# A ring of transfers moved from unrolled code into a hardware loop, and three loops placed differently in instruction memory

## Chip, cores, metric

One core of one Trainium2 chip. The time is device microseconds (us) of one execution; lower is better. "Before" is the kernel before the change, "after" the changed one.

## The reference

```python
def reference(x):                       # x: (4, 4096, 4352) float32
    B, N, D = x.shape
    G = 8
    x_g = x.reshape(B, N, G, D // G)
    x_g = x_g - x_g.max(axis=-1, keepdims=True)
    exp = np.exp(x_g)
    out = exp / exp.sum(axis=-1, keepdims=True)
    return out.reshape(B, N, D).astype(np.float32)
```

A softmax over groups of 544 numbers, 16,384 x 8 of them. It reads 285 MB and writes 285 MB.

## The kernel before

64 tiles of 128 partitions x 2 rows (4352 KB, 34,816 contiguous bytes a partition) go through a ring of six buffers and are worked on in place. SyncE issues all transfers from unrolled code; VectorE takes the maxima and scales, ScalarE exponentiates and sums. A "row" s is half a tile; the loops of ScalarE and VectorE have one body for the 12 rows of the ring.

```python
    def loop(engine):
        return nc.Fori(
            0, turns, engines=OrderedEngineSet([engine.engine]), head_slot={engine.engine: 0})
    # ... [vector_max, vector_scale, scalar_exp: cut]
    def load(t):
        b = t % NT                                   # NT = 6
        if t >= NT:
            nc.sync.wait_ge(stored[b], 16 * (t // NT))
        nc.sync.dma_start(out=bufs[b][:, :], in_=xt[t]).then_inc(landed[b], 16)

    def store(t):
        nc.sync.wait_ge(scaled, R * (t + 1))         # R = 2
        nc.sync.dma_start(out=ot[t], in_=bufs[t % NT][:, :]).then_inc(stored[t % NT], 16)

    for t in range(NT - 1):
        load(t)
    for t in range(nt):                              # nt = 64, unrolled
        store(t)
        if t + NT - 1 < nt:
            load(t + NT - 1)
    # ... [final waits: cut]
    with loop(nc.scalar):
        for s in range(S):                           # S = 12
            scalar_exp(s)
    # ... [last 8 rows unrolled: cut]
    vector_max(0)
    with loop(nc.vector):
        for s in range(S):
            vector_max((s + 1) % S)
            vector_scale(s)
```

`head_slot` says at which slot of a block of instruction memory the loop's first instruction is put. If the code ahead ends elsewhere, the engine jumps over the gap: VectorE's loop, put at slot 0 before and nowhere in particular after, has 12 branch records in the trace of before, one of them at 14.34 us where it enters the loop.

## Time and profile before

| | before |
|---|---|
| time, median (range) | 1330.28 us (1330.23 to 1330.37) |
| span in the profile | 1329.4 us |
| bytes moved | 570.43 MB, DMA engines 99.5% busy |
| busy VectorE, ScalarE | 78%, 57% |
| instruction packets in the span | 8 |

The lines are in the prediction below. One measure used throughout is not in a view, so here is how it is made. The 128 transfers leave 2048 landing records, 16 each. The page counts 16 DMA engines, and I take each record as the landing of one engine's part. I sort the 16 records of a transfer and take the last minus the eighth. I call this the **lag**: how far the latest DMA engine is behind the bulk. The records don't say which engine left them; that a late engine is the same one from transfer to transfer is read from its lag moving smoothly. These records, and the single instructions and packets named below without a view, stand in the packed trace.

### The profile page before, as it was taken

Reading aid. Unit: us, or ns where it says so; the run is one execution under the profiler, and the core shown is the slowest. Engines: PE = TensorE matmul, PEld = TensorE weight load, DVE = VectorE, ACT = ScalarE, POOL = GpSimd, SP = SyncE. Lnnn points to the kernel's source line nnn. Section 1 sums busy time; section 2 is a strip of 40 time slices with the busy share of each in tenths; the row PEclk is TensorE's granted clock in tenths of the full one; section 3 lists DMA queues with packets and bytes.
Section 4 is the critical chain, followed back from the end, with each engine's and each line's share of the span. In section 5 each row is a group of like instructions: output and inputs, shape, how many; then the busy total and the mean of one; then the engine's idle time right before and its main releaser. Section 6 shows DMA issues by size and latency. Waiting matters only on the chain. (4 is left out here: it accounts for less than half of the span.)

```text
span 1329.4 us, 4004 instructions
## 1 busy us (share of the span) xinstructions
DVE 1041.5 (78%) x1280; ACT 764.4 (57%) x2049; POOL 0.2 (0%) x4
## 2 busy tenths in 40 slices
DVE  5999987787877878778787787787877878778771
ACT  3777765655656556565565555655656556555560
POOL 0000000000000000000000000000000000000000
DMA  9999999999999999999999999999999999999997
GB/s 402 420 433 434 434 429 432 431 434 432 435 435 429 433 431 434 434 435 435 433 433 431 432 435 435 436 433 433 427 435 435 436 436 432 432 429 435 434 436 323
DMA packets 18440, 570.50 MB, mean 429 GB/s; under 512 B 2048, under 2 KB 2048, under 8 KB 2048
## 3 DMA queue, kind: packets, MB, share of 16 engines
q1 hardware_dynamic: 18432, 570.43, 99.5%
q14 instruction: 8, 0.07, 0.0%
HBM read 285.21 MB, written 285.21 MB: 429 GB/s over the span
## 5 line engine op out<-in xcount | busy, mean ns | idle before, releaser
L77 ACT ACTIVATE xt<-xt,mx 128x544 f32<-128x544 f32 x1024 | 751.2, 734 | 530.4 <-ACTq L74 530.4
L61 DVE TENSOR_REDUCE mx<-xt 128x8 f32<-128x4352 f32 x128 | 599.1, 4680 | 235.8 <-DVEq L60 234.8
L69 DVE TENSOR_SCALAR xt<-xt,rs 128x544 f32<-128x544 f32 x1024 | 434.0, 497 | 19.2 <-DVEq L66 0.9
L77 ACT ACTIVATION_READ_ACCUMULATOR xt<-xt,mx 128x1 f32 x1024 | 191.1, 187 | 0.0
L65 DVE RECIPROCAL rs<-sm 128x8 f32<-128x8 f32 x128 | 24.5, 191 | 3.2 <-DVEq L64 3.2
L107 ACT ACT_TABLE_LOAD x1 | 1.3, 1283 | 0.9 <-SPq L43 0.9
L138 POOL MEMSET const-bfloat16-1.0<- 128x1 bf16 x1 | 0.1, 102 | 0.0
L138 POOL MEMSET const-uint8-127<- 128x1 uint8 x1 | 0.1, 102 | 0.0
L138 POOL MEMSET const-float32-0.0<- 128x1 f32 x1 | 0.1, 99 | 0.2 <-issue 0.2
L138 POOL MEMSET const-float32-1.0<- 128x1 f32 x1 | 0.1, 99 | 0.0
## 6 DMA issues: line engine op xcount, KB each, us to landing
xt<-in_x_dram SPq DMA_DIRECT2D x64, 4352.0 KB, 30.8
out_dram<-xt SPq DMA_DIRECT2D x64, 4352.0 KB, 40.8
```

Source lines behind the costliest of these rows:

```text
L61: nc.vector.reduce_max(out=mx[:, s, :], in_=row(s), axis=X, negate=True).then_inc(max_done, 1)
L65: nc.vector.reciprocal(out=rs[:, s, :], in_=sm[:, s, :]).then_inc(rec_done, 1)
L69: i = nc.vector.tensor_scalar_mul(out=xr[:, g, :], in0=xr[:, g, :], scalar1=rs[:, s, g:g + 1])
L77: i = nc.scalar.activation(out=xr[:, g, :], in_=xr[:, g, :], func=Exp, bias=mx[:, s, g:g + 1], scale=1.0, accum_out=sm[:, s, g:g + 1],)
L107: nc.scalar.preload_act_table(Exp)
L138: nc = _bacc.Bacc("TRN2", target_bir_lowering=False, num_devices=1)
```

## The change

The intent, as I read it: SyncE's program gets shorter (54 unrolled steps become 9 turns of 6), ScalarE's loop is put just behind the code that leads into it, and VectorE's lies wherever it falls.

```diff
+    AHEAD = NT - 1
+    ring_turns = (nt - AHEAD) // NT
+    # ... [turn_in, turn_out: the rows of one turn, indexed by the loop variable: cut]
+    def take(engine, sem, n=1):
+        engine.sem_inc(sem, -n).wait_op(sem, n, "sem-ge")
-    def load(t):
-        b = t % NT
-        if t >= NT:
-            nc.sync.wait_ge(stored[b], 16 * (t // NT))
-        nc.sync.dma_start(out=bufs[b][:, :], in_=xt[t]).then_inc(landed[b], 16)
+    # ... [the new load(t, source) and store(t, target), which waits with take(): cut]
+    def step(t, source, target):
+        store(t, target)
+        take(nc.sync, stored[(t - 1) % NT], 16)
+        load(t + AHEAD, source)
     # ... [the unrolled calls of load and store of before: cut]
+    nc.sync.sem_inc(stored[NT - 1], 16)
+    for t in range(AHEAD):
+        load(t, xt[t])
+    with nc.Fori(
+            0, ring_turns, engines=OrderedEngineSet([nc.sync.engine]),
+            head_slot={nc.sync.engine: 0}) as u:
+        for t in range(NT):
+            step(t, turn_in[u, t], turn_out[u, t])
+    # ... [the last 10 tiles unrolled: cut]
-    with loop(nc.scalar):
+    with nc.Fori(
+            0, turns, engines=OrderedEngineSet([nc.scalar.engine]),
+            head_slot={nc.scalar.engine: 54}):
-    with loop(nc.vector):
+    with nc.vector.Fori(0, turns):
```

More of the change, by code (lines that the diff above doesn't have):

```diff
@@ L34 @@
     ot = of.rearrange("(t p r) d -> t p (r d)", p=P, r=R)
+    AHEAD = NT - 1
+    ring_turns = (nt - AHEAD) // NT
+    steps = ring_turns * NT
+    turn_in = xf[AHEAD * P * R:(AHEAD + steps) * P * R, :].rearrange(
+        "(u b p r) d -> u b p (r d)", b=NT, p=P, r=R)
+    turn_out = of[:steps * P * R, :].rearrange("(u b p r) d -> u b p (r d)", b=NT, p=P, r=R)
     landed = [tc.alloc_semaphore(f"landed{b}") for b in range(NT)]
@@ L47 @@
     rs = ctx.enter_context(nc.sbuf_tensor("rs", [P, S, G], f32))
-    def loop(engine):
-        return nc.Fori(
-            0, turns, engines=OrderedEngineSet([engine.engine]), head_slot={engine.engine: 0})
+    def take(engine, sem, n=1):
+        engine.sem_inc(sem, -n).wait_op(sem, n, "sem-ge")
     def row(s):
@@ L59, in vector_max @@
         if s % R == 0:
-            nc.vector.sem_inc(landed[s // R], -16).wait_op(landed[s // R], 16, "sem-ge")
+            take(nc.vector, landed[s // R], 16)
         nc.vector.reduce_max(out=mx[:, s, :], in_=row(s), axis=X, negate=True).then_inc(max_done, 1)
     def vector_scale(s):
-        nc.vector.sem_inc(exp_done, -1).wait_op(exp_done, 1, "sem-ge")
+        take(nc.vector, exp_done)
         nc.vector.reciprocal(out=rs[:, s, :], in_=sm[:, s, :]).then_inc(rec_done, 1)
-        nc.vector.sem_inc(rec_done, -1).wait_op(rec_done, 1, "sem-ge")
+        take(nc.vector, rec_done)
         xr = row(s)
@@ L73, in scalar_exp @@
     def scalar_exp(s):
-        nc.scalar.sem_inc(max_done, -1).wait_op(max_done, 1, "sem-ge")
+        take(nc.scalar, max_done)
         xr = row(s)
@@ L85, in scalar_exp, with load, store @@
         i.then_inc(exp_done, 1)
-    def load(t):
-        b = t % NT
-        if t >= NT:
-            nc.sync.wait_ge(stored[b], 16 * (t // NT))
-        nc.sync.dma_start(out=bufs[b][:, :], in_=xt[t]).then_inc(landed[b], 16)
-    def store(t):
-        nc.sync.wait_ge(scaled, R * (t + 1))
-        nc.sync.dma_start(out=ot[t], in_=bufs[t % NT][:, :]).then_inc(stored[t % NT], 16)
-    for t in range(NT - 1):
-        load(t)
-    for t in range(nt):
-        store(t)
-        if t + NT - 1 < nt:
-            load(t + NT - 1)
-    for b in range(NT):
-        nc.sync.wait_ge(stored[b], 16 * ((nt - b + NT - 1) // NT))
+    def load(t, source):
+        nc.sync.dma_start(out=bufs[t % NT][:, :], in_=source).then_inc(landed[t % NT], 16)
+    def store(t, target):
+        take(nc.sync, scaled, R)
+        nc.sync.dma_start(out=target, in_=bufs[t % NT][:, :]).then_inc(stored[t % NT], 16)
+    def step(t, source, target):
[10 more added lines that the diff above has]
+            step(t, turn_in[u, t], turn_out[u, t])
+    for t in range(ring_turns * NT, nt):
+        if t + AHEAD < nt:
+            step(t, xt[t + AHEAD], ot[t])
+        else:
+            store(t, ot[t])
+    for t in range(nt - NT, nt):
+        nc.sync.wait_ge(stored[t % NT], 16)
     nc.scalar.preload_act_table(Exp)
-    with loop(nc.scalar):
+    with nc.Fori(
+            0, turns, engines=OrderedEngineSet([nc.scalar.engine]),
+            head_slot={nc.scalar.engine: 54}):
         for s in range(S):
```

## The prediction

> **What bounds the kernel now.** I read the page first: the engines' shares, the slices, the DMA queues.
>
> ```profile
> DVE 1041.5 (78%) x1280; ACT 764.4 (57%) x2049; POOL 0.2 (0%) x4
> ...
> DMA  9999999999999999999999999999999999999997
> GB/s 402 420 433 434 434 429 432 431 434 432 435 435 429 433 431 434 434 435 435 433 433 431 432 435 435 436 433 433 427 435 435 436 436 432 432 429 435 434 436 323
> ...
> q1 hardware_dynamic: 18432, 570.43, 99.5%
> q14 instruction: 8, 0.07, 0.0%
> ```
>
> No compute engine is full, while the 16 DMA engines are full in every slice but the last. 570.43 MB at the 435 GB/s of the good slices take 1311 us; the time is 1330. What any change can gain without moving fewer bytes is the other 19 us: a weaker first two slices (402 and 420 GB/s: 33.2 us x (33 + 15)/435 = 3.7 us), a weak last one (323: 33.2 x 112/435 = 8.5 us), and a few tenths in each of the rest.
>
> Next, the waits of SyncE, because SyncE issues all transfers and is the engine that the change rewrites.
>
> ```profile
> SPq L92 <- DMA out_dram<-xt: 1141.8, 58, 21.3
> SPq L96 <- DVE xt L69: 102.0, 6, 33.3
> ```
>
> 58 of the 59 waits before a load are for an earlier store to land; only six stores (start and end) wait for VectorE. So the ring turns at the pace of the transfers. The timeline of SyncE in the middle gives the beat:
>
> ```profile
> 649.16 0.33 SPq L92 DMA_DIRECT2D xt<-in_x_dram  x1
> 649.53 0.46 SPq L96 DMA_DIRECT2D out_dram<-xt  x1
> 669.73 0.33 SPq L92 DMA_DIRECT2D xt<-in_x_dram  x1
> 670.10 0.48 SPq L96 DMA_DIRECT2D out_dram<-xt  x1
> ```
>
> One load and one store in 20.57 us, 10.28 us a transfer (128 of them: 1316 us); SyncE issues both in 0.83 us and sleeps for the rest. How deep is the queue when it wakes? The issues say:
>
> ```profile
> xt<-in_x_dram SPq DMA_DIRECT2D x64, 4352.0 KB, 30.8
> out_dram<-xt SPq DMA_DIRECT2D x64, 4352.0 KB, 40.8
> ```
>
> A load lands 30.8 us after issue, three transfers of 10.28; the store issued just behind it 40.8, four. So when store t-1 lands and SyncE wakes, load t+4 and store t are still queued, about 20.5 us of work. A late SyncE costs nothing until it is about 20 us late.
>
> The same for compute: in the trace VectorE ends tile 30 at 626.8 and its store is issued at 649.5, so a finished tile waits 22.7 us for SyncE. VectorE has two free gaps a tile as well:
>
> ```profile
> 659.57 4.69 DVE L61 TENSOR_REDUCE mx<-xt 128x8 f32<-128x4352 f32 x1 [4.01 <-DVEq L60]
> ```
>
> Last, the end of the kernel, in windows of two us (columns: busy VectorE, ScalarE, GpSimd, clock, DMA share, GB/s):
>
> ```profile
> 1318.00:1320.00 2.00, 0.00 (x0) 0.00 (x0) 0.00 (x0) 1.00 0.73 313
> 1320.00:1322.00 2.00, 0.00 (x0) 0.00 (x0) 0.00 (x0) 1.00 0.24 104
> 1322.00:1324.00 2.00, 0.00 (x0) 0.00 (x0) 0.00 (x0) 1.00 0.28 122
> 1324.00:1326.00 2.00, 0.00 (x0) 0.00 (x0) 0.00 (x0) 1.00 0.16 70
> 1326.00:1328.00 2.00, 0.00 (x0) 0.00 (x0) 0.00 (x0) 1.00 0.04 17
> ```
>
> From 1321 to 1329 us a quarter of the DMA engines or fewer still move bytes. The sixteen landing records of each transfer say why: twelve come within 0.4 us, four come late, in the last transfer by 5.2, 6.4, 6.6 and 7.6 us. Over the run the latest one's lag behind the bulk grows from 0.7 us (first transfer) over 4.3 (at 117 us) to 7.4 (at 508 us), and then stays at 7.6. These four engines end the kernel. It is the only term of size that a change in instruction fetch could reach.
>
> [...] there are 8 fetch packets of 0.07 MB, about 8 KB[...] each, and none repeats with the turns of the two loops, so both bodies stay resident.[...]
>
> **The change part by part.**
>
> *SyncE.* It removes 54 unrolled steps and puts them in 9 turns of 6. Order is the same: store t, wait for store t-1, load t+5. The waits on rising counts become decrements by what was waited for; the extra 16 put on the last buffer's semaphore only lets step 0 pass, where the old code did not wait. Added: one semaphore instruction before the first load; address arithmetic for 12 transfers a turn; 8 taken branches. I take the address arithmetic as at most 1 us a transfer (an estimate, above twice the 0.33 to 0.48 us of a whole issue here), so at most 2 us a step[...]. Against 20.5 us of queued work: cost 0. Entering the loop at slot 0 of a block may fetch one or two blocks, after the five loads went out (0.95 to 3.9 us) and before the first store (37.2 us): 0 as well. On the path: the one instruction before the first load[...].
>
> *ScalarE.* Same instructions, other position. Its body is 12 x (1 + 8 x 2) + 2 = 206 slots (each activation is a pair: 1024 ACTIVATE and 1024 READ_ACCUMULATOR in the groups). At slot 0 it fills two pieces of 128; at 54 it ends at 260 and touches a third. The intent, I think, is that 54 lies just behind the code before the loop, so that entering needs no fetch. ScalarE enters before 19 us, where it waits for the first maximum anyway: 0.
>
> *VectorE.* Same instructions; body 12 x 12.5 + 2 = 152 slots, now wherever the code before it ends. Before, entering the aligned loop had a visible gap:
>
> ```profile
> 19.85 4.69 DVE L61 TENSOR_REDUCE mx<-xt 128x8 f32<-128x4352 f32 x1 [0.93 <-issue]
> ```
>
> and a fetch packet stands just before it, at 18.0 us after the start. If the new loop lies in blocks already loaded, these 0.93 us go, at a time when VectorE leads the first three stores: they come about 0.9 us earlier. But five loads of 10.3 us are queued until about 56 us and the first store is issued at 37.2, so the transfers don't notice: 0.
>
> *The fetches as DMA work.* One 8 KB packet takes 0.3 to 0.8 us of one DMA engine, and the data packet behind it takes 0.3 to 0.6 us longer, about 0.9 us of lag each. Which engine carries which packet the trace doesn't say. Fewer fetches (ScalarE's and VectorE's four at entry, SyncE's at 757 us) minus up to two new ones for SyncE: about three less, at most 3 x 0.9 = 2.7 us if all were on the latest engine and nothing refilled the lag. The lag, though, went on growing between 130 and 500 us with no fetch in that time, and then stood still, so something else feeds it up to a level. I count a fifth of it: -0.5 us.
>
> Sum: +0.05 + 0 + 0 + 0 - 0.5 = about -0.5 us on 1330.3: 1329.8 us.
>
> **The rivals.** *A: refetch on every turn.* If the third piece of ScalarE's body (slots 256 to 259), or VectorE's straddling body, throws the first piece out, each of 10 turns fetches 2 to 4 pieces: 20 to 40 packets x 0.9 us, 18 to 36 us more for one DMA engine. It is hidden from the compute engines (22.7 us of slack a tile), but the DMA engine itself has none: 1345 to 1360 us if all of it shows. For it: the body does grow by a piece[...]. Against it: before, VectorE ran into its second piece (a fetch at 109.9 us, when its first turn reaches slot 128) and nothing was fetched at the back edge, so at least three pieces are held. I give it 10%, and less than full size when it comes.
>
> *B: the lag of the four engines goes or grows.* Its level of 7.6 us may hang on how SyncE's two issues lie against each other (0.37 us apart now, a different gap in the loop). If it vanished: 1322.7 us. If it grew by half: 1334. For it: the growth without fetches had a period of about 20.5 us, the ring's. Against: it stands still for 800 us, so it looks set by the transfers.
>
> *C: SyncE becomes late.* A fetch stall at each back edge plus address arithmetic would have to reach 20 us in one step. Nothing in the timeline is within a factor of five of this. The time stays.
>
> *D: other descriptors.* If addresses in registers split the transfers otherwise, the rate changes. Queue 1 is already of the dynamic kind, rows and strides are the same (34,816 contiguous bytes a partition). I give it 1%.
>
> **Range and chances.** The middle is a ceiling of bytes that the change doesn't touch; what moves is the tail of 7.6 us and a start of tenths. B's ordinary variation, 3 to 4 us each way, sets the range: 1326 to 1334 us. Faster by over 2% would be under 1303.7, below 1311 us of bytes at the ceiling: 0.5%. Slower by over 2% is over 1356.9: rival A at nearly full size, or D: 2%. Within 2%: 97.5%.
>
> **What would show it.** Right: slices at 433 to 436 GB/s, queue 1 still 18432 packets, SyncE still waiting over 1100 us for stores, landings of 30.8 and 40.8 us, few instruction packets, the gap of 0.93 us at VectorE's second maximum gone, the last slice within 300 to 400 GB/s. Wrong by A: instruction packets in the tens and more and a longer weak end. By B: the late engines' lag other than 7.6 us, and the time moved by just that. By C: SyncE's waits for stores shrink and DMA shares fall under 0.98 in the middle. By D: another packet count or landing time.

Two terms: one is 0.1 us for a branch, which counted as 0 under the 20.5 us of queued work. The other is +0.05 us for the one semaphore instruction before the first load; the line of the sum has it. With both, the sum came to about -0.5 us on 1330.3, so 1329.8 us.

Two words need their measure. The "ceiling" is the rate of the best slices, 435 to 436 GB/s with the DMA engines 99.5% busy; that nothing could go faster was not shown. A "piece" is what one instruction packet brings, 8192 bytes. That it holds 128 slots is my reading. The trace of before goes with it: the packets at 79.0 and 109.9 us start when ScalarE has 131 and VectorE 135 instruction records since entering its loop, not far past 128.

## The result, and the profile after

After: 1332.62 us median (1332.17 to 1333.15), before beside it 1330.26 us (1329.78 to 1330.37). The ratio is 1.0019, 95% interval 1.0001 to 1.0036. The change is a slowdown of about 2.4 us: within 2%, and inside the range, but on the other side of zero from the -0.5 us that I had summed up.

The page after, the slices and the queues:

```profile
GB/s 400 419 434 433 433 433 433 433 428 431 432 434 433 435 434 435 433 430 430 433 433 434 433 435 435 435 430 430 432 432 435 434 432 435 435 434 430 430 431 308
...
q1 hardware_dynamic: 18432, 570.43, 99.4%
q14 instruction: 9, 0.07, 0.0%
...
xt<-in_x_dram SPq DMA_DIRECT2D x64, 4352.0 KB, 30.7
out_dram<-xt SPq DMA_DIRECT2D x64, 4352.0 KB, 40.5
```

The middle has hardly moved: same packets, 428 to 435 GB/s, landing times within 0.3 us. Only the last slice is weaker, 308 in place of 323. The timeline of SyncE after, at the same place as before:

```profile
649.06 0.34 SPq L93 DMA_DIRECT2D xt<-in_x_dram  x1
649.97 0.35 SPq L97 DMA_DIRECT2D out_dram<-xt  x1
669.71 0.34 SPq L93 DMA_DIRECT2D xt<-in_x_dram  x1
670.30 0.35 SPq L97 DMA_DIRECT2D out_dram<-xt  x1
```

The beat is 20.65 us here (20.57 before) and the tick came at 649.06 (649.16 before). The store follows its load after 0.59 us, or 0.91 once a turn at the jump back, in place of 0.37 us. So the loop does cost SyncE some 0.2 to 0.5 us a step, under 20 us of queued work, where it costs nothing.

The end of the two kernels in windows (DMA share and GB/s are the last two columns), first before:

```profile
1320.00:1324.00 4.00, 0.00 (x0) 0.00 (x0) 0.00 (x0) 1.00 0.26 113
1324.00:1328.00 4.00, 0.00 (x0) 0.00 (x0) 0.00 (x0) 1.00 0.10 44
1328.00:1332.00 4.00, 0.00 (x0) 0.00 (x0) 0.00 (x0) 1.00 0.01 2
```

then after:

```profile
1320.00:1324.00 4.00, 0.00 (x0) 0.00 (x0) 0.00 (x0) 1.00 0.26 113
1324.00:1328.00 4.00, 0.00 (x0) 0.00 (x0) 0.00 (x0) 1.00 0.16 70
1328.00:1332.00 4.00, 0.00 (x0) 0.00 (x0) 0.00 (x0) 1.00 0.02 9
```

The bulk of the DMA engines runs dry at the same time; a few run on longer. The landing records give the size: the eighth landing of the last transfer is at 1320.54 us before and 1320.55 us after, the last one 7.43 us behind it before and 9.49 us after. The whole of the 2.0 us between the two spans is lag.

Where does the lag come from? After, it is 2.1 us in the first transfer (before 0.65), and the three late engines behind the latest one flatten out too, though only by about 1100 us. The latest itself climbs steadily, 0.37 us in 100 us (7.69 us at transfer 81, 8.91 at transfer 113, 329 us later). In before one late engine climbs like that too, but from 0.35 us at 179 us, so that it is still under the latest at the end (6.2 us at transfer 127, the latest 7.4). I call this engine the climbing one. The start looks different as well, in the DMA view of 5 to 15 us. Before:

```profile
q1 hardware_dynamic: 144, 4.46, 103.3%
q14 instruction: 1, 0.01, 0.2%
```

and after:

```profile
q1 hardware_dynamic: 140, 4.35, 101.4%
q14 instruction: 3, 0.02, 0.6%
```

Queue 14 brings instructions (its kind on the page). Two packets more, at 7.6 and 13.3 us: after SyncE's five loads are out, when it enters its loop. Each took 0.31 us, and one data packet starts within 0.01 us of its end and takes longer than the usual 1.29 us (1.61 and 1.70), so I read that it went through one DMA engine. The packed trace has the jump itself: SyncE's branch stands at 3.59 us and the loop's first instruction at 9.16 us, 5.6 us later. At each jump back it is 0.16 us.

### The profile page after: what moved, and what is told of

The parts are those of the page before. It is cut to its first block, busy times and chain, and to the rows that moved or that the text cites. A ratio compares the mean times of both kernels' runs of the same rounds, so it can differ in the third digit from the quotient of the medians.

```text
span 1331.4 us, 4367 instructions
## 1 busy us (share of the span) xinstructions
DVE 1041.6 (78%) x1280; ACT 764.4 (57%) x2049; POOL 0.2 (0%) x4
```

## The experiments

**The theories.** *F (fetch):* jumping to slot 0 of a new block makes SyncE fetch two pieces of 8 KB at 8 and 14 us. They go through one DMA engine, put it behind at the start, and since this engine keeps falling behind by 0.37 us in 100 us, it ends last. *I (issue):* the loop's issues, with addresses from registers and a wider gap between load and store, feed the lag throughout. *P (placement of the others):* ScalarE's and VectorE's new places do it. *R* in the first batch is "SyncE's loop, by F or I". The runs come on different chips, so each is read against the runs of before on its own chip.

Lags are those of the profiled run. "Entry packets" are the extra two in 5 to 15 us.

| kernel | us, median (range) | ratio to before, 95% | entry packets | lag, first / last transfer | span | span - last lag |
|---|---|---|---|---|---|---|
| before | 1330.28 (1330.23 to 1330.37) | | no | 0.65 / 7.43 | 1329.43 | 1322.0 |
| after | 1332.62 (1332.17 to 1333.15) | 1.0019 (1.0001 to 1.0036) | yes | 2.11 / 9.49 | 1331.37 | 1321.9 |
| 1 SyncE loop alone | 1332.04 (1331.78 to 1332.59) | 1.0018 (1.0004 to 1.0031) | yes | 1.36 / 8.38 | 1330.24 | 1321.9 |
| 2 ScalarE alone | 1329.60 (1329.01 to 1329.86) | 0.9997 (0.9983 to 1.0011) | no | 0.70 / 6.12 | 1328.06 | 1321.9 |
| 3 VectorE alone | 1329.70 (1329.16 to 1331.04) | 1.0004 (0.9990 to 1.0018) | no | 0.55 / 4.93 | 1327.37 | 1322.4 |
| 4 after, SyncE unrolled | 1330.17 (1330.04 to 1331.21) | 1.0006 (0.9992 to 1.0020) | no | 1.07 / 6.16 | 1328.24 | 1322.1 |
| 5 after, SyncE loop not placed | 1329.95 (1329.75 to 1330.06) | 1.0000 (0.9987 to 1.0014) | no | 0.89 / 6.03 | 1328.14 | 1322.1 |
| 6 after, unrolled but placed | 1332.98 (1332.61 to 1333.73) | 1.0024 (1.0010 to 1.0037) | yes | 1.40 / 9.32 | 1331.63 | 1322.3 |
| 7 after, SyncE at slot 64 | 1330.24 (1329.60 to 1330.92) | 1.0004 (0.9990 to 1.0018) | no | 0.60 / 5.71 | 1327.82 | 1322.1 |
| 8 after, a second jump late | 1333.74 (1333.68 to 1334.03) | 1.0029 (1.0016 to 1.0043) | yes, and two at 1150 us | 1.74 / 9.92 | 1331.97 | 1322.1 |
| 11 after again | 1332.51 (1331.88 to 1332.85) | 1.0021 (1.0008 to 1.0034) | yes | 1.35 / 8.04 | 1330.10 | 1322.1 |

The last column is the strongest line: in eleven profiles the span is 1321.9 to 1322.4 us plus the lag, whatever the kernel (runs 9, 10 and 12 split the last store and are told further down). The times of profiled runs lie about 1.8 us above their spans (1333.15 over 1331.4). The one profile of before was of one of its longer executions (1331.24 us): its median of 1329.9 us on a later chip corresponds to a lag near 6 us (1329.9 - 1.8 - 1322.1).

### 1 to 4: which part does it

```diff
# 1: the changed kernel, but
-            head_slot={nc.scalar.engine: 54}):
+            head_slot={nc.scalar.engine: 0}):
-    with nc.vector.Fori(0, turns):
+    with nc.Fori(0, turns, engines=OrderedEngineSet([nc.vector.engine]),
+            head_slot={nc.vector.engine: 0}):
# 2: the kernel before, with ScalarE's head_slot 54
# 3: the kernel before, with nc.vector.Fori(0, turns) on VectorE
# 4: the changed kernel, with load, store and the unrolled ring of before
```

Expected of 1: 

> SyncE's ring in a loop at slot 0, ScalarE and VectorE as in the kernel before. Theory R (the ring's loop makes the latest DMA engine later, by its instruction fetches near the start or by its later issues): about +2 us, 1332 to 1333, and the latest engine 9 us or more behind the bulk in the last transfer. Theory P (the new places of ScalarE's and VectorE's loops do it): 1330.3 within 0.5, lag about 7.6 us.

Expected of 2: 

> The kernel before with ScalarE's loop at slot 54 and nothing else. Theory R: 1330.3 within 0.5 us. Theory P: up to +2 us, from the third piece of 128 slots that its body now touches. Rival refetch on every turn: instruction packets above 20; the changed kernel had 9, so I expect 8 or 9.

Expected of 3: 

> The kernel before with VectorE's loop unaligned and nothing else. Theory R: 1330.3 within 0.5 us, perhaps 0.5 us less since two early fetch packets go. Theory P: up to +2 us. The gap of 0.93 us at VectorE's second maximum goes.

Expected of 4: 

> The changed kernel with SyncE unrolled again as before. Theory R: 1330.3 within 0.7 us or a little faster, lag at the end 6 to 7.6 us. Theory P: 1332.5 within 0.5 us, lag 9 us or more.

Measured: SyncE's part alone costs 2.2 us by the medians (1332.04 against 1329.84), and its interval keeps clear of 1. The three kernels with SyncE unrolled are as before. P falls. My rival of the prediction, a refetch on every turn, falls too: 9 packets in ten turns with ScalarE's loop at slot 54, though its body then touches three pieces. In run 1 the lag was 8.4 us at the end, a little under the 9 that I expected of it. In run 3 the gap at VectorE's second maximum is closed, and the time doesn't notice. The two packets that VectorE's own jump to slot 0 brings in before, at 18.0 and 24.0 us, are gone there as well, and the time doesn't notice that either: not any two packets cost 2 us.

### 5 to 7: the loop, or the jump into it

Loop and placement are two things. After has both and before has neither; 4 is without both too. Run 5 has the loop alone, run 6 the placement alone.

```diff
# 5: the changed kernel, but
-    with nc.Fori(0, ring_turns, engines=..., head_slot={nc.sync.engine: 0}) as u:
+    with nc.sync.Fori(0, ring_turns) as u:
# 6: run 4's unrolled SyncE, but
+    with nc.Fori(0, 1, engines=OrderedEngineSet([nc.sync.engine]),
+            head_slot={nc.sync.engine: 0}):     # one turn: the jump alone
         for t in range(nt):
             store(t)
             ...
# 7: the changed kernel, but
-            head_slot={nc.sync.engine: 0}) as u:
+            head_slot={nc.sync.engine: 64}) as u:
```

Expected of 5: 

> The changed kernel with SyncE's loop where the code before it ends, so that entering it needs no jump. Theory F (the block fetches at the jump put the DMA engine that carries SyncE's instructions behind at the start, and it keeps falling behind by 0.38 us in 100 us until the end): no SyncE packets near 8 and 14 us, the latest engine 5 to 6.5 us behind at the end, time 1329 to 1330, as fast as the kernel before or half a us faster. Theory I (the loop's issues, with addresses from registers, feed the lag): 1332 to 1333, lag 8 us or more, as placed.

Expected of 6: 

> SyncE unrolled as before, but the unrolled part put behind a jump to slot 0 of a new block (a loop of one turn), ScalarE and VectorE as in the changed kernel. Theory F: packets near 8 and 14 us, the engine with the steady growth is the latest from the start, lag 9 us or more, 1332 to 1333.5. Theory I: 1330.2 as with SyncE unrolled and not placed, lag about 6 us.

Expected of 7: 

> The changed kernel with SyncE's loop at slot 64 in place of 0: placed, but most likely inside the block that is loaded already (its 38 instructions then end at 102). Theory F: as the unplaced loop, 1329 to 1330 and lag 5 to 6.5 us. If placing itself costs, or theory I: 1332 to 1333.

Measured: the loop without the jump is as fast as before (ratio 1.0000); the jump without the loop costs 1.0024. On one chip in the same rounds the slowest of run 5 is 1330.06 us and the fastest of run 6 is 1332.61 us. F holds, and I falls. The DMA view of 5 to 15 us, run 5 first:

```profile
q14 instruction: 1, 0.01, 0.2%
```

and run 6:

```profile
q14 instruction: 3, 0.02, 0.6%
```

and run 7:

```profile
q14 instruction: 1, 0.01, 0.2%
```

The end in windows, run 5:

```profile
1320.00:1324.00 4.00, 0.00 (x0) 0.00 (x0) 0.00 (x0) 1.00 0.30 131
1324.00:1328.00 4.00, 0.00 (x0) 0.00 (x0) 0.00 (x0) 1.00 0.02 9
1328.00:1332.00 4.00, 0.00 (x0) 0.00 (x0) 0.00 (x0) 1.00 0.00 0
```

and run 6:

```profile
1320.00:1324.00 4.00, 0.00 (x0) 0.00 (x0) 0.00 (x0) 1.00 0.28 122
1324.00:1328.00 4.00, 0.00 (x0) 0.00 (x0) 0.00 (x0) 1.00 0.08 35
1328.00:1332.00 4.00, 0.00 (x0) 0.00 (x0) 0.00 (x0) 1.00 0.03 11
```

The tail follows the two packets and not the loop. Run 7 was meant to add that placing as such is harmless, and can't: its trace has no jump into SyncE's loop, and the same numbers of SyncE's instructions of each kind as run 5, so it repeats run 5 (1330.24 us, a little over the 1330 expected). The body has 50 instructions a turn in the trace, not the 38 of my expectation. That the fetch counts, and not the jump, has to come from run 8 and from a fetch without a jump in before, both told next.

### 8: double the suspected cost

```diff
# the changed kernel, but
+    with nc.Fori(0, 1, engines=OrderedEngineSet([nc.sync.engine]),
+            head_slot={nc.sync.engine: 0}):
         for t in range(ring_turns * NT, nt):
             ...
```

Expected: 

> The changed kernel with a second jump to slot 0 of a new block on SyncE, ahead of its last ten tiles (about 1150 us). Theory F: one or two more packets there, each with 0.5 to 0.9 us for the latest engine, so lag 10 to 11.5 us and 1333 to 1334.5. Theory I: 1332.6, nothing added.

Measured: two more packets, at 1148.3 and 1154.1 us, as the DMA view of 1143 to 1159 us shows:

```profile
q14 instruction: 2, 0.02, 0.2%
```

The time is 1333.74 us, a ratio of 1.0029 where after has 1.0019 and 1.0021. These intervals overlap and the chips differ, so the step inside the trace has to carry this point. The latest engine's lag is 7.75 us at 1084 us and 9.36 at 1167, up 1.61; after rises 0.31 in the same stretch. So two packets cost this engine 1.3 us, 0.65 each. The trace shows the parts: each packet took 0.31 us, and the data packets behind them took 1.70 and 1.56 us in place of 1.29. The two entry packets of after have the same size: the data packets behind them took 1.61 and 1.70 us, 1.36 us for both in all. Since they hit the very engine that was last, SyncE's instructions come through the engine that climbs. The kernel before agrees: SyncE's unrolled code fetches once in mid-run, at 756.8 us, without any jump (after, with the loop, has no packet from 115 to 1254 us), and it is the climbing engine that goes from 3.55 to 4.36 us there, from one transfer to the next. The lag at the end, 9.92 us, came just short of the 10 to 11.5 expected.

### 9, 10 and 12: sharing out the tail, and a mistake

If a few engines end late, could the others take some of the last store? Run 9 splits it by rows, into 96 and four times 8, to give some engines more rows and others fewer. Which rows run on which engine was my assumption; no run shows it. Run 10 is the control, 96 and 32 rows, by which nothing was meant to be shifted. Both are run 5 with this edit (and the final wait raised to match):

```diff
+            for lo, hi in TAIL:   # 9: (0,96),(96,104),(104,112),(112,120),(120,128); 10: (0,96),(96,128)
+                nc.sync.dma_start(out=ot[t][lo:hi, :], in_=bufs[t % NT][lo:hi, :]).then_inc(...)
```

Expected of 9: 

> Unplaced SyncE loop, and the last store split: 96 rows[...], then 4 stores of 8 rows[...]. If the late engines are all among the relieved ones: 1327 to 1327.8. If one of the latest is among the loaded ones: 1331 to 1332.6.[...]

Expected of 10: 

> Control for the split: the last store as 96 rows and 32 rows[...]. Nothing is shifted: 1329.5 to 1330.3, like the unplaced loop alone.

Measured: 1341.12 us (1.0085) and 1340.59 us (1.0073; 1334.59 to 1340.95). Both far outside what I expected, the control as much as the trial, so run 9 says nothing about where the late engines are. The end of run 10 in windows:

```profile
1320.00:1324.00 4.00, 0.00 (x0) 0.00 (x0) 0.00 (x0) 1.00 0.78 261
1324.00:1328.00 4.00, 0.00 (x0) 0.00 (x0) 0.00 (x0) 1.00 0.21 70
1328.00:1332.00 4.00, 0.00 (x0) 0.00 (x0) 0.00 (x0) 1.00 0.16 70
1332.00:1336.00 4.00, 0.00 (x0) 0.00 (x0) 0.00 (x0) 1.00 0.06 26
```

From 1305 us on, a packet of 34,816 bytes takes 1.58 us in the mean and up to 5.1, in after again 1.29 at most. Is it the cut by rows, or a second store as such? Run 12 tests it by cutting columns instead, three quarters and one quarter, so that each store has all 128 rows.

Expected of 12: 

> The unplaced SyncE loop with the last store split by columns, three quarters and one quarter of each row, all 128 rows in both. If splitting by rows was slow[...]: no packet slowed, 1329.5 to 1330.5, like the unplaced loop alone. If a second store at the end costs by itself: 1335 to 1341 as with the split by rows.

Measured: 1330.41 us (1329.97 to 1331.22), ratio 0.9998. A second store at the end costs nothing when it is cut by columns; it is the cut by rows that costs about 10 us (1340.59 and 1341.12 us). Why, no run shows.

### 11: after once more

Expected: 

> The changed kernel once more, beside the others: 1332 to 1333, a ratio of 1.002 to the kernel before; the latest engine 9 us or more behind at the end, growing by 0.35 to 0.4 us in 100 us after 400 us.

Measured: 1332.51 us, 1.0021, and the climb of the latest engine is 0.38 us in 100 us (6.22 us at transfer 81, 7.47 at 113). Its lag at the end, 8.0 us, is under the 9 that I expected: it varies by more than 1 us from run to run, and the span with it.

No version beat the kernel before. Run 5 keeps the loop at no cost and is the one to take if the shorter program is wanted.

## Why the prediction was right and where it failed

- *The bound.* Right: the middle is the bytes, moved at 427 to 436 GB/s before and 428 to 435 after, and the bulk of the DMA engines ended at 1320.5 us in both kernels.
- *Slips of reading.* SyncE has 58 waits before a load and all are for a store: the ring has 59 loads, and the first doesn't wait. Rival A's 18 to 36 us more would be 1348 to 1366 us, not 1345 to 1360.
- *SyncE's loop costs 0.* Right for the loop (run 5), by the step given: 20 us of queued work above it. My 2 us a step was too high; the gap from load to store grew from 0.37 us to 0.59 and at most 0.91. The jump back, the prediction's 0.1 us, is 0.16 us from the branch to the next instruction on SyncE. The one semaphore instruction before the first load, +0.05 us in the sum, has a record of 17 ns in after, and the first load is issued at 1.05 us in place of 0.95.
- *ScalarE and VectorE cost 0.* Right (runs 2 to 4). The gap of 0.93 us did close, as the timeline after shows:

```profile
15.95 9.28 DVE L65 TENSOR_REDUCE mx<-xt 128x8 f32<-128x4352 f32 x2 [15.95 <-DVEq L56]
```

- *The first stores come 0.9 us earlier.* Wrong: the first store is issued at 39.1 us, before at 37.2, since the first tile landed later (VectorE starts at 15.95 us, before at 14.24): its last part was 2.11 us behind the eighth, in place of 0.65. That it costs nothing was right.
- *"Entering the loop at slot 0 of a block may fetch one or two blocks ... 0 as well".* **This step failed.** I booked the fetch as time of SyncE, which sleeps there, and took it off the path. It is work of a DMA engine as well (0.31 us a packet, and 0.3 to 0.4 us more for the data packet behind it), and the DMA engines, 99.5% busy, are the path: with the two packets the kernel takes 2.2 to 3.3 us longer by the medians (after, runs 1, 6 and 11, each against before), without them it is as fast as before (runs 5 and 7). Of this, 1.3 us is what two packets cost their engine directly; the rest is growth of the early delay, which no run explains. That the measured time lies in the range is no support for this step: the range is 8 us wide and takes in either sign.
- *The fetches as DMA work, -0.5 us.* The size of a packet was near (0.9 us estimated, 0.65 measured in run 8) and the sign wrong. I expected about three packets fewer in all and counted them as alike. There were 9 in place of 8, and it matters which engine they hit and when: the one that takes SyncE's never stops climbing, so what it gets early stays until the end (9.5 us behind at transfer 127 in after, 6.2 in before).
- *The lag "then stood still, so something else feeds it up to a level".* Half right. It holds for most of the late engines, which flatten between 1 and 7.4 us. I looked only at the latest and missed the one still climbing below it.
- *Rival B, the time moves by just the lag.* Right: +2.06 us of lag, +1.94 us of span. But its supposed handle, the gap between the issues, is not it (run 5). Rivals A, C and D did not show.

**Open.** What feeds the climb of one engine: about seven of its 16 packets a step take 3 to 28 ns longer, before and after alike, whether SyncE runs from a loop or not. Why a few engines fall behind in the first 400 us (in after until about 1100 us) and then stop. And why an early delay grows: at transfer 17 the climbing engine is 4.1 us behind in after and about 0.35 in before, though its two packets cost it 1.4 us. The latest engine's lag as such goes from 0.65 us in the first transfer to 4.7 by the 17th in before, and from 2.1 to 4.1 in after. The late engines' numbers are not in the trace.

## What to carry to other kernels

In this kernel, bound by its transfers, the last DMA engine set the end (the span is 1321.9 to 1322.4 us plus its lag). What went through one DMA engine counted, instruction fetches too, even where the engine that waits for them sleeps anyway: SyncE's two packets at the entry came with 2.2 to 3.3 us more, while without VectorE's two the time was the same (run 3, ratio 1.0004). So put a loop on the issuing engine where entering it fetched nothing, as in run 5; aligning it to slot 0 was not free here. And sort the last landings of a trace, transfer by transfer, before calling the tail a property of the bytes.
